# Starting the next pass in the first half of a gated-MLP unit: a two-layer decoder trunk on one core

## The chip, the cores and the metric

The kernel runs on one core of one Trainium2 chip. The metric is the device time of one execution in microseconds (us). Two layers run on 256 tokens, everything in 32-bit floats, with weights streamed once from memory.

## What is computed

Each of two layers is a mixer (gated spatial mixing and a gated recurrence in layer 0, forgetting attention in layer 1) followed by the gated MLP that the change is about:

```
def conv_ffn(h, w_up, conv_w, conv_b, w_down):
    seq = h.shape[1]
    z = h @ w_up                                   # 2048 -> 2 x 5632
    zp = jnp.pad(z, ((0, 0), (CONV_WIDTH - 1, 0), (0, 0)))
    z = sum(conv_w[j] * zp[:, j:j + seq] for j in range(CONV_WIDTH)) + conv_b
    a, b = jnp.split(z, 2, axis=-1)
    return (jax.nn.silu(a) * b) @ w_down           # 5632 -> 2048
```

with `x = x + conv_ffn(rms_norm(x), ...)` around it.

## The kernel before

**Numbers.** Every 32-bit factor is split into a high part and a remainder, and a product is three matmuls: high by high, high by remainder, remainder by high. For weights the split is done on the fly: a load of 512 KB on SyncE's queue (`weights`, L199) fills a buffer `w` (five of them), ScalarE copies its high part to `wh` (L186), VectorE subtracts to `wl` (L187), and TensorE may run.

**Pieces.** `project_four` makes four output blocks of 128 columns at a time for all 256 tokens, into two PSUM banks (one for each 128 tokens). It walks the inner dimension in *pieces* of 256: one load, one high part, one remainder, twelve matmuls of 512 columns (L380, L382, L383). Ahead of each piece it calls `tick()`, which moves a few waiting generators one step on; that is how evacuation, convolution and the rest are threaded between pieces.

**Ups.** `ffn` is a row of eleven *ups* a layer. An up makes four hidden tiles: its **first half** (`za`, the silu side) and its **second half** (`zb`, the linear side), each a `project_four` over 2048. After a half, `empty` evacuates two banks with the row scale (ScalarE L1422, into `z`), VectorE transposes in 32x32 blocks (L483), and 16 small moves of 32 KB, half on SyncE's queue and half on GpSimd's (L492), put the blocks in place in `zt`. Then `empty` lets LATE = 8 ticks go by before the convolution `conv` takes one of its four tiles at each tick: one tap with bias on ScalarE (L1436), one tap on ScalarE (L1437, into `tmp`), the middle tap on VectorE (L1438); then a closing add of all four (L1440). The first half ends with a silu, the second with the product of both sides (L1462) and a split into `hid` (L1466, L1468).

**Downs.** After three or two ups (STEPS) a *down* multiplies the hidden tiles made so far by `w_down`, in four `project_four` q = 0 to 3, added up in `y` (L1598, L1600). Ups run one or two ahead of what the down needs.

**The inset.** The first pieces of two neighbouring `project_four` (both halves of an up, or two q of a down) are done together by `seven`: seven block products (21 matmuls, L435 to L437) in place of eight (24 matmuls), at the price of sums of weights on VectorE (L448 to L451), of three and a half more weight splits, of sums of activations made once for each pass (`combos` in `combine`, L395 to L407), of two copies of a bank on ScalarE (L457, L462) and of two adds from PSUM on VectorE (L465, L470). `seven` is a generator in five steps and a rest: its two loads (L445), the sums, then the products. `project_four` drives it as its `inset`, one step ahead of each piece from the third on; two of its steps call `tick()` as well. It writes the four banks with which the next up or the next two q begin; those then skip their first piece ("begun").

**Where it stands.** In `up` the inset is handed to the second half: its seven pieces run with the start of the next up, or of the down when the up is the last before one. So a first half has 7 ticks (8 if not begun) and a second half 9. `combine(k0)` for a down is put in the queue of generators ahead of the last up before that down.

**Banks.** All eight PSUM banks are in use, four called `pm` and four `px`. `two_banks` hands out pairs, two pairs from one pool and two from the other in turn, so the four banks of a unit are a mixed set.

**Order.** The framework plans an order for each engine: by program order, but what it thinks is ready earlier may pass what it thinks is not. `held(r)` forbids `r` to go ahead of the last high part (or remainder) of a piece issued so far; it adds no wait on another engine. On the chip each engine then runs its instructions in that order, and waits where an operand is not there.

Of the kernel before, what the change touches and what calls it, by code (L numbers as in the profile page):

```python
# [8 lines left out]
F32 = mybir.dt.float32  # L9
# [6 lines left out]
P = 128  # L16
S = 256
D = 2048
KT = D // P
# [4 lines left out]
STEPS = ((3, 1), (3, 1), (3, 2), (2, 0))  # L24
BLK = 32
LAG = 6
LATE = 8
FORGET = 4
PAIR = 5
WAIT = 4  # L30
# [26 lines left out]
def tile_trunk(ctx: ExitStack, tc: tile.TileContext, x, pp_d, cst_d, mlev_d, msk_d,  # L57
# [295 lines left out]
                    deep["last"] = PE.matmul(to_two(ps[T]), al, h, start=False, stop=k + i == KT - 1)  # L353
        return ps

    def two_banks():
        ring[0] += 2
        pick = (lambda: pm.tile([P, 512], F32, tag="pm", name=nm("pm"))) if ring[0] % 8 < 4 else bank
        return [pick() for _ in range(2)]

    ring = [0]
    def project_four(w4, acts, n, k0=0, ks=None, ps=None, more=False, inset=None):

        begun = ps is not None
        loose = begun and "seven" in deep
        ps = ps or (two_banks() if "seven" in deep else
                    [pm.tile([P, 512], F32, tag="pm", name=nm("pm")) for _ in range(2)])
        ks = ks or range(0, n, 2)
        for k in ks:
            if inset is not None and (k - ks[0]) // 2 >= inset[1]:  # L370
                next(inset[0], None)
            tick()
            lo = (k0 + k) * P
            wh, wl = weights(w4[:, :, lo:lo + 2 * P].rearrange("m p c -> p m c"), 1024, 4)
            for T in range(2):
                for i in range(2):
                    a = acts(k + i) if callable(acts) else acts[k + i]
                    ah, al = a[:, T * P:(T + 1) * P], a[:, S + T * P:S + (T + 1) * P]
                    h, l = (by_rows(t, i) for t in (wh, wl))
                    PE.matmul(to_rows(ps[T]), ah, h, start=not begun and k + i == ks[0], stop=False,  # L380
                              skip_group_check=loose)
                    PE.matmul(to_rows(ps[T]), ah, l, start=False, stop=False, skip_group_check=loose)  # L382
                    deep["mm"] = deep["last"] = PE.matmul(to_rows(ps[T]), al, h, start=False,  # L383
                                                          stop=not more and k + i == ks[-1] + 1,
                                                          skip_group_check=loose)
        if inset is not None and inset[2]:
            for _ in inset[0]:
                pass
        return ps
# [1009 lines left out]
    def ffn(l, norm, last):  # L1399
# [10 lines left out]
            return (hp.tile([P, 1024], F32, tag="tmp", name=nm("tmp"), bufs=2),  # L1410
                    hp.tile([P, 4, S], F32, tag="zt", name=nm("zt"), bufs=2))

        def four(j0, inset=None, ps=None):
            ps = project_four(w_up[l, j0:j0 + 4], A, KT, ks=range(2 if ps else 0, KT, 2), ps=ps, inset=inset)
            tmp, zt = room()

            def empty():
                while norm.Rt is None:
                    yield
                z = [hp.tile([P, 512], F32, tag="z", name=nm("z"), bufs=2) for _ in range(2)]  # L1420
                for T in range(2):
                    SC.activation(cols4(z[T]), of_rows(ps[T]), AF.Copy, scale=norm.Rt[:, T:T + 1])  # L1422
                transposed(lambda T: z[T], tmp, zt)
                for _ in range(LATE):
                    yield

            return zt, tmp, empty()

        def conv(z4, tmp, j):
            c = hp.tile([P, 4, S], F32, tag="conv", name=nm("conv"), bufs=2)  # L1430
            far = tmp.rearrange("p (m t) -> p m t", m=4)
            for i in range(4):
                w = [pp[:, o:o + 1] for o in (C_CW + (l * 3 + n) * 2 * HT + j + i for n in range(3))]
                cb = C_CB + l * 2 * HT + j + i
                z, ci = z4[:, i], c[:, i]
                held(SC.activation(ci, z, AF.Identity, bias=pp[:, cb:cb + 1], scale=w[2]))  # L1436
                SC.activation(far[:, i], z, AF.Copy, scale=w[0])  # L1437
                V.scalar_tensor_tensor(ci[:, 1:], z[:, :S - 1], w[1], ci[:, 1:], ALU.mult, ALU.add)  # L1438
                yield
            held(V.tensor_tensor(c[:, :, 2:], c[:, :, 2:], far[:, :, :S - 2], ALU.add), "wl")  # L1440
            return c

        def up(j0, inset=None, begun=()):
            pa, pb = begun or (None, None)
            za, ta, ea = four(j0, None, pa)
            ca = []

            def gate():
                yield from ea
                a = yield from conv(za, ta, j0)  # L1450
                yield
                held(act(a, a, AF.Silu))
                ca.append(a)

            start(gate())
            zb, tb, eb = four(HT + j0, inset, pb)

            def fill():
                yield from eb
                b = yield from conv(zb, tb, HT + j0)  # L1460
                yield
                held(V.tensor_tensor(b, b, ca[0], ALU.mult), "wl")  # L1462
                t = hp.tile([P, 4, 512], F32R, tag="hid", name=nm("hid"), bufs=5)
                h, lo = (t[:, :, i * S:(i + 1) * S].rearrange("p m (t n) -> p m t n", t=2) for i in range(2))
                src = view(b, 0, (S, 4), (1, 2), (2, P))
                SC.activation(h, src, AF.Copy)  # L1466
                yield
                held(V.tensor_tensor(lo, src, h.bitcast(F32), ALU.subtract), "wl")  # L1468
                hid.extend(t[:, i] for i in range(4))

            start(fill())
# [68 lines left out]
        def begin(w4s, k, acts):  # L1540
            got = []

            def banks4():
                got.extend((two_banks(), two_banks()))
                return got

            def sums():
                while comb[0] != k:
                    tick()
                return right  # L1550

            spare = hp.tile([P, 512], F32, tag="z", name=nm("p5"), bufs=2)
            return got, seven(w4s, acts, lambda: comb[1], (k or 0) * P, banks4, sums, spare)
# [7 lines left out]
        def down(k0, n, first, final, begun, after):  # L1561
# [3 lines left out]
            for q in range(4):  # L1565
                if last and final and q == 3:
                    parts = None
                    for m in range(4 * q, KT):
                        end = m == KT - 1
                        ps = project(w_dn[l, m], acts, chunks=(n,), k0=k0, parts=parts)  # L1570
                        if not end:
                            tick()
                            parts = weights(w_dn[l, m + 1][:, k0 * P:(k0 + n) * P], n * P)
                        V.tensor_tensor(xT[m], xT[m], ps[:, 0:S], ALU.add)
                        finish_x(m)
                    return
                inset = ps = ks = None
                if not final:
                    ps, ks = begun[q % 2], range(2, n, 2)
                    if q == 0:  # L1580
                        later, gen = begin_down(2, k0)
                        inset = (gen, 2, False)
                    elif q == 1:
                        inset = (gen, 0, True)
                    elif q == 3 and after:
                        coming, gen = begin_up(j0)
                        inset = (gen, 0, True)
                ps = project_four(w_dn[l, 4 * q:4 * q + 4], acts, n, k0, ks=ks, ps=ps, inset=inset)
                if q == 1 and not final:
                    begun = later  # L1590
                    if after:
                        queue.append(combine(None))
                    else:
                        x_back()
                for T in range(2):
                    d = y[:, T, q * 512:(q + 1) * 512]
                    if first:
                        SC.activation(cols4(d), of_rows(ps[T]), AF.Copy)  # L1598
                    else:
                        V.tensor_tensor(cols4(d), cols4(d), of_rows(ps[T]), ALU.add)  # L1600
                if final:
                    add_y(q, True)
# [5 lines left out]
        for g, (now, ahead) in enumerate(STEPS):  # L1608
            until = sum(n for n, _ in STEPS[:g + 1]) + ahead
            while j0 < until:  # L1610
                now_begun, begun, inset = begun, (), None
                if j0 + 1 == until:
                    queue.append(combine(k0))
                    begun, gen = begin_down(0, k0)
                    inset = (gen, 2, True)
                elif j0:
                    begun, gen = begin_up(j0 + 1)
                    inset = (gen, 2, True)
                up(4 * j0, inset, now_begun)
                j0 += 1  # L1620
            n, final = 4 * now, g == len(STEPS) - 1
            while len(hid) < k0 + n:
# [94 lines left out]
```

## Time and profile before

| | |
|---|---|
| device time, median of 3 runs | 2194.82 us (2188.66 to 2194.99) |
| the profiled execution, its own time | 2194.9 us |
| its span, first to last instruction | 2193.1 us |
| VectorE busy | 1750.2 us (80%) |
| ScalarE busy | 1428.8 us (65%) |
| bytes moved, mean rate | 491.99 MB, 224 GB/s |
| the gated MLP's weight loads, issued | 346.8 to 1038.6 us (layer 0), 1483.4 to 2176.1 us (layer 1) |

A row of the windows view gives a stretch in us from the span's start, its length, and the busy time of each engine with the number of its instructions in brackets. A row of the timeline gives start, duration, engine, line and operands; in square brackets stands how long the engine sat idle before it, and what ended that. A row of the waits view gives who waited for whom: us in total, times, longest. TensorE's matmuls overlap: each is shown with some 0.38 us while they start 0.22 us apart, so its busy share says little about small losses.

### The profile page before, as it was taken

The numbers are of one execution on the slowest core, as the hardware profiler recorded it, in microseconds if no ns is written. First come the engines' busy times: TensorE is split into PE (matmuls) and PEld (weight loads), VectorE is DVE, ScalarE is ACT, GpSimd is POOL, SyncE is SP. The second block draws the span as 40 slices with busy tenths as digits, with TensorE's granted clock in tenths as the row PEclk, the third lists the DMA queues.
The fourth block names the chain that finished last, engine by engine and source line by source line (L and its number), as shares of the span: only waits on it lengthen the run. The fifth ranks groups of instructions, "written<-read, shape, count | busy, mean of one in ns | idle before, by whom it ended". The sixth has DMA issues, their size and how long they took to land.

```text
span 2193.1 us, 32450 instructions
## 1 busy us (share of the span) xinstructions
PE 2158.5 (98%) x10646; PEld 1879.4 (86%) x10646; DVE 1750.2 (80%) x2373; ACT 1428.8 (65%) x2064; POOL 480.6 (22%) x873
## 2 busy tenths in 40 slices
PE   9999999999999999999999999999999999999999
PEld 8888888888888887888888888888788888888888
DVE  7888768778768967886987887877788778877986
ACT  6677766676667656774666556766677567657762
POOL 0352231212012001210233443222121021011202
PEclk9999999999999999999999999999999999999999
DMA  8755778867777766677777766787777767677796
GB/s 297 220 173 174 230 222 263 241 190 209 231 218 222 233 221 192 208 242 243 250 238 222 242 206 207 217 264 235 217 220 232 238 190 223 205 224 231 208 289 190
DMA packets 494345, 491.99 MB, mean 224 GB/s; under 512 B 115584, under 2 KB 460304, under 8 KB 494048
## 3 DMA queue, kind: packets, MB, share of 16 engines
q1 hardware_dynamic: 466752, 457.60, 66.6%
q0 software_dynamic: 25984, 30.18, 5.7%
q10 hardware_dynamic: 1440, 2.15, 0.3%
q8 instruction: 83, 1.36, 0.3%
q14 instruction: 86, 0.70, 0.1%
HBM read 439.44 MB, written 6.31 MB: 203 GB/s over the span
## 4 chain that ended last, share of the span: by engine, by line
PE 72%; DVE 10%; DMA 9%; SPq 4%; issue 3%; ACT 2%; DVEq 0%; POOL 0%; ACTq 0%; POOLq 0%
PE pm L382 11%; PE pm L380 11%; PE pm L383 11%; DMA w<-in_w_up 6%; PE px L382 5%; PE px L383 5%; PE px L380 5%; DVE wl L187 5%; PE pm L351 4%; PE pm L353 4%; PE pm L352 4%; SPq L492 3%; DMA w<-in_w_dn 2%; DVE tmp L483 1%; PE pm L237 1%
## 5 line engine op out<-in xcount | busy, mean ns | idle before, releaser
L187 DVE TENSOR_TENSOR wl<-w,wh 128x1024 fp32r<-128x1024 f32 (+1 forms) x790 | 950.4, 1217 | 319.1 <-ACT wh L186 317.4
L186 ACT ACTIVATE wh<-w 128x1024 fp32r<-128x1024 f32 (+1 forms) x790 | 818.2, 1049 | 466.8 <-PE pm L383 132.5
L492 POOL DMA_DIRECT2D zt<-tmp x413 | 224.3, 551 | 1143.4 <-DVE tmp L483 836.7
L382 PE MATMUL pm<-wl,a 128*128 128x512 f32 x952 | 364.2, 383 | 8.2 <-DVE wl L187 8.2
L380 PE MATMUL pm<-wh,a 128*128 128x512 f32 x952 | 363.1, 381 | 0.1
L383 PE MATMUL pm<-wh,a 128*128 128x512 f32 x952 | 361.9, 380 | 0.0
L382 PE MATMUL px<-wl,a 128*128 128x512 f32 x632 | 241.5, 382 | 5.6 <-DVE wl L187 5.5
L380 PE MATMUL px<-wh,a 128*128 128x512 f32 x632 | 240.3, 380 | 0.0
L383 PE MATMUL px<-wh,a 128*128 128x512 f32 x632 | 240.0, 380 | 0.0
L382 PEld LDWEIGHTS pm<-wl,a 128*128 128x128 f32 x952 | 180.7, 190 | 39.4 <-DVE wl L187 14.2
L380 PEld LDWEIGHTS pm<-wh,a 128*128 128x128 f32 x952 | 180.5, 190 | 26.3 <-ACT wh L186 0.5
L383 PEld LDWEIGHTS pm<-wh,a 128*128 128x128 f32 x952 | 180.8, 190 | 25.4
L351 PE MATMUL pm<-wh,a 128*128 128x512 f32 x416 | 158.5, 381 | 0.0
L352 PE MATMUL pm<-wl,a 128*128 128x512 f32 x416 | 157.7, 379 | 0.0
L353 PE MATMUL pm<-wh,a 128*128 128x512 f32 x416 | 157.7, 379 | 0.0
L382 PEld LDWEIGHTS px<-wl,a 128*128 128x128 f32 x632 | 119.9, 190 | 27.5 <-DVE wl L187 10.7
L1436 ACT ACTIVATE conv<-zt,pp 128x256 f32<-128x256 f32 x176 | 104.8, 595 | 52.2 <-DMA zt<-tmp 38.4
L380 PEld LDWEIGHTS px<-wh,a 128*128 128x128 f32 x632 | 120.0, 190 | 17.2
L383 PEld LDWEIGHTS px<-wh,a 128*128 128x128 f32 x632 | 119.7, 189 | 16.8
L492 POOL DMA_DIRECT2D turn<-tmp x159 | 86.7, 553 | 184.1 <-DVE tmp L483 162.4
L382 PE MATMUL px<-wl,hid 128*128 128x512 f32 x304 | 115.6, 380 | 0.7 <-DVE wl L187 0.7
L187 DVE TENSOR_TENSOR wl<-sums,wh 128x1024 fp32r<-128x1024 f32 (+1 forms) x90 | 94.2, 1046 | 26.8 <-ACT wh L186 26.8
(334 smaller groups left out, 3949.8 us busy)
## 6 DMA issues: line engine op xcount, KB each, us to landing
w<-in_w_up SPq DMA_DIRECT2D x334, 512.0 KB, 5.9
w<-in_w_dn SPq DMA_DIRECT2D x164, 512.0 KB, 5.6
w<-in_w_cqkv SPq DMA_DIRECT2D x96, 512.0 KB, 5.2
w<-in_w_abo SPq DMA_DIRECT2D x32, 512.0 KB, 5.0
w<-in_w_cg SPq DMA_DIRECT2D x32, 512.0 KB, 5.5
w<-in_w_co SPq DMA_DIRECT2D x32, 512.0 KB, 5.3
zt<-tmp SPq DMA_DIRECT2D x416, 32.0 KB, 2.2
zt<-tmp POOLq DMA_DIRECT2D x413, 32.0 KB, 2.0
```

The source lines that it names most:

```text
L186: r = deep["wh"] = SC.activation(wh, w, AF.Copy)
L187: deep["wl"] = V.tensor_tensor(wl, w, wh.bitcast(F32), ALU.subtract)
L237: deep["last"] = PE.matmul(to_two(ps[g][T]), a[:, o + T * P:o + (T + 1) * P], by_two(t, i), start=k + i + j == 0, stop=k + i == KT - 1 and ...
L351: PE.matmul(to_two(ps[T]), ah, h, start=k + i == 0, stop=False)
L352: PE.matmul(to_two(ps[T]), ah, l, start=False, stop=False)
L353: deep["last"] = PE.matmul(to_two(ps[T]), al, h, start=False, stop=k + i == KT - 1)
L380: PE.matmul(to_rows(ps[T]), ah, h, start=not begun and k + i == ks[0], stop=False, skip_group_check=loose)
L382: PE.matmul(to_rows(ps[T]), ah, l, start=False, stop=False, skip_group_check=loose)
L383: deep["mm"] = deep["last"] = PE.matmul(to_rows(ps[T]), al, h, start=False, stop=not more and k + i == ks[-1] + 1, skip_group_check=loose)
L483: r = V.transpose(tmp.rearrange("p (b m i t) -> p b m i t", b=4, m=4, t=2)[:, :, :, :, T], src(T).rearrange("p (m b j) -> p b m j", m=4, b=4))
L492: queues[(a + b) % len(queues)].dma_start(dst[BLK * b:BLK * (b + 1), :, a * n:(a + 1) * n], tmp[BLK * a:BLK * (a + 1), b * 4 * n:(b + 1) * ...
L1436: held(SC.activation(ci, z, AF.Identity, bias=pp[:, cb:cb + 1], scale=w[2]))
```

## The change

The inset moves from the second half of an up to the first. All four banks of an up are taken at its start, and banks are handed out by fours, all `pm` or all `px` in turn; a `project_four` that gets fresh banks is told so (`fresh`). The combination for a down is put in the queue in the middle of the second-last up before it, behind its inset, and no longer at the start of the last up. The convolution waits nine ticks, not eight. The ScalarE tap L1437 is held like L1436.

```diff
-LATE = 8
+LATE = 9
...
-    def two_banks():
-        ring[0] += 2
-        pick = (lambda: pm.tile([P, 512], F32, tag="pm", name=nm("pm"))) if ring[0] % 8 < 4 else bank
-        return [pick() for _ in range(2)]
+    def four_banks():
+        ring[0] += 1
+        pick = (lambda: pm.tile([P, 512], F32, tag="pm", name=nm("pm"))) if ring[0] % 2 else bank
+        return [[pick() for _ in range(2)] for _ in range(2)]
...
-    def project_four(w4, acts, n, k0=0, ks=None, ps=None, more=False, inset=None):
-
-        begun = ps is not None
+    def project_four(w4, acts, n, k0=0, ks=None, ps=None, more=False, inset=None, fresh=False):
+
+        begun = ps is not None and not fresh
         loose = begun and "seven" in deep
-        ps = ps or (two_banks() if "seven" in deep else
-                    [pm.tile([P, 512], F32, tag="pm", name=nm("pm")) for _ in range(2)])
+        ps = ps or [pm.tile([P, 512], F32, tag="pm", name=nm("pm")) for _ in range(2)]
...
-        def four(j0, inset=None, ps=None):
-            ps = project_four(w_up[l, j0:j0 + 4], A, KT, ks=range(2 if ps else 0, KT, 2), ps=ps, inset=inset)
+        def four(j0, inset, ps, begun):
+            ps = project_four(w_up[l, j0:j0 + 4], A, KT, ks=range(2 if begun else 0, KT, 2), ps=ps, inset=inset,
+                              fresh=not begun)
...
-                SC.activation(far[:, i], z, AF.Copy, scale=w[0])
+                held(SC.activation(far[:, i], z, AF.Copy, scale=w[0]))
...
-        def up(j0, inset=None, begun=()):
-            pa, pb = begun or (None, None)
-            za, ta, ea = four(j0, None, pa)
+        def up(j0, inset=None, begun=(), after=None):
+            pa, pb = begun or four_banks()
+            za, ta, ea = four(j0, inset, pa, begun)
+            if after is not None:
+                queue.append(after)
...
-            zb, tb, eb = four(HT + j0, inset, pb)
+            zb, tb, eb = four(HT + j0, None, pb, begun)
...
-                got.extend((two_banks(), two_banks()))
+                got.extend(four_banks())
...
-                inset = ps = ks = None
+                inset = ks = None
+                if not q % 2:
+                    pair = begun or four_banks()
+                ps = pair[q % 2]
                 if not final:
-                    ps, ks = begun[q % 2], range(2, n, 2)
+                    ks = range(2, n, 2)
...
-                now_begun, begun, inset = begun, (), None
+                now_begun, begun, inset, then = begun, (), None, None
                 if j0 + 1 == until:
-                    queue.append(combine(k0))
                     begun, gen = begin_down(0, k0)
                     inset = (gen, 2, True)
                 elif j0:
                     begun, gen = begin_up(j0 + 1)
                     inset = (gen, 2, True)
-                up(4 * j0, inset, now_begun)
+                if j0 + 2 == until:
+                    then = combine(k0)
+                up(4 * j0, inset, now_begun, then)
```

More of the change, by code (lines that the diff above doesn't have):

```diff
@@ L1587, in down @@
                         inset = (gen, 0, True)
-                ps = project_four(w_dn[l, 4 * q:4 * q + 4], acts, n, k0, ks=ks, ps=ps, inset=inset)
+                ps = project_four(w_dn[l, 4 * q:4 * q + 4], acts, n, k0, ks=ks, ps=ps, inset=inset,
+                                  fresh=final)
                 if q == 1 and not final:
```

## The prediction

> **What bounds the kernel now.** I begin with the page's first part, then ask who made TensorE wait.
>
> ```profile
> PE 2158.5 (98%) x10646; PEld 1879.4 (86%) x10646; DVE 1750.2 (80%) x2373; ACT 1428.8 (65%) x2064; POOL 480.6 (22%) x873
> ```
> ```profile
> PE pm L382 <- DVE wl L187: 8.7, 11, 2.3
> PE px L435 <- ACT px L457: 8.5, 2, 4.7
> PE px L382 <- DVE wl L187: 6.3, 8, 1.6
> PE pm L435 <- ACT pm L457: 3.6, 3, 2.6
> ```
>
> TensorE has nearly no room: the change takes no matmul away, so all it can win is waits. They are of two kinds: a matmul with a weight remainder waits for VectorE (8.7 + 6.3 us), and a product of the inset waits for ScalarE's copy L457 (8.5 + 3.6 us). Both lie in the ups. How much an up loses in all, a window from evacuation to evacuation shows better, because a busy matmul is drawn with 0.38 us and issued every 0.216:
>
> ```profile
> 788.00:827.90 39.90, 39.90 (x186) 34.95 (x185) 27.92 (x32) 23.97 (x30) 4.34 (x8) 1.00 0.74 234
> ```
> ```profile
> 402.03:452.64 50.61, 47.50 (x210) 40.37 (x209) 38.92 (x46) 33.48 (x49) 8.70 (x16) 0.97 0.72 216
> ...
> 492.05:537.09 45.04, 42.74 (x190) 36.82 (x189) 37.66 (x49) 31.08 (x44) 8.69 (x16) 0.96 0.70 210
> ...
> 827.90:875.72 47.82, 43.17 (x190) 37.18 (x189) 35.23 (x41) 30.90 (x42) 8.69 (x16) 0.93 0.73 219
> ...
> 1538.16:1590.27 52.11, 47.51 (x210) 40.38 (x209) 38.88 (x46) 33.62 (x48) 8.70 (x16) 0.97 0.69 210
> ...
> 2045.81:2087.44 41.63, 41.28 (x191) 35.60 (x190) 36.78 (x48) 30.96 (x45) 8.69 (x16) 1.00 0.65 192
> sum 696.01, PE 671.94 PEld 578.18 DVE 567.51 ACT 493.87 POOL 139.03; mean PE 42.00 PEld 36.14 DVE 35.47 ACT 30.87 POOL 8.69
> ```
>
> The first fence is the first up behind a down: 186 matmuls, no idle, so 39.90 / 185 = 0.2157 us from start to start. It and its three sisters lose nothing. The second fence is the other sixteen ups with an inset: 696.01 us for 3065 matmuls (210, 181, then 190 or 191 each, in both layers). Less one at each window's edge, 3049 x 0.2157 = 657.7 us: the **pool is 38.3 us**. Three windows hold half of it: 50.61 - 45.1 = 5.5, 47.82 - 40.8 = 7.0 and 52.11 - 45.1 = 7.0, together **19.5**; thirteen others share **18.8**, of which the one at 492 has 4.3.
>
> Now the halves of two ups (first half of the up at work, second, and again):
>
> ```profile
> 638.90:661.00 22.10, 22.10 (x104) 19.36 (x103) 13.66 (x16) 13.41 (x19) 4.34 (x8) 1.00 0.63 189
> 661.00:681.50 20.50, 19.08 (x88) 16.17 (x87) 20.35 (x24) 16.79 (x25) 4.34 (x8) 1.00 0.77 237
> 681.50:704.30 22.80, 22.80 (x107) 19.96 (x107) 16.62 (x25) 14.63 (x21) 4.34 (x8) 1.00 0.73 224
> 704.30:724.40 20.10, 18.50 (x86) 15.65 (x85) 20.07 (x24) 16.39 (x25) 4.34 (x8) 1.00 0.50 141
> ```
>
> The fourth figure is VectorE: 13.66 of 22.10 and 16.62 of 22.80 in first halves, 20.35 of 20.50 and 20.07 of 20.10 in second halves. Over an up VectorE has room; in the half with the inset it has none, and there TensorE idles.
>
> The three dear windows have another cause, on ScalarE (timeline, then TensorE's for the same place, then for the window at 492):
>
> ```profile
> 865.00 0.60 ACT L1436 ACTIVATE conv<-zt,pp 128x256 f32<-128x256 f32 x1 [5.34 <-DMA zt<-tmp]
> 865.51 0.49 ACT L1437 ACTIVATE tmp<-zt,pp 128x256 f32<-128x256 f32 x1
> 865.91 1.04 ACT L186 ACTIVATE wh<-sums 128x1024 fp32r<-128x1024 f32 x1
> 866.85 0.58 ACT L457 ACTIVATE px<-px 128x512 f32<-128x512 f32 x1
> ```
> ```profile
> 867.48 0.80 PE L435 MATMUL px<-wh,a 128*128 128x512 f32 x1 [4.65 <-ACT px L457]
> 868.07 0.63 PE L436 MATMUL px<-wl,a 128*128 128x512 f32 x1
> 868.50 0.63 PE L437 MATMUL px<-wh,a 128*128 128x512 f32 x1
> ```
> ```profile
> 523.01 0.48 PE L382 MATMUL pm<-wl,a 128*128 128x512 f32 x1 [2.30 <-DVE wl L187]
> ...
> 524.32 0.63 PE L383 MATMUL pm<-wh,a 128*128 128x512 f32 x1
> ```
>
> The first convolution tap of the first half's tiles stands at the eighth tick, ahead of two instructions of the inset that need nothing from it. Its `zt` has not landed, ScalarE sits 5.34 us, and the copy L457 with TensorE behind it waits. After such a stop matmuls start 0.43 us apart for some 4 us (868.07, 868.50): a second bill of about 2 us.
>
> The Trainium skill, page "TensorE: Matmul & The Clock Gate", Part 1, puts the half rate behind an idle window of about 3.4 us. The row at 523.01 shows it already after 2.30 us; by the rule that window would win some 2 us less than I credit, by the row it wins them.
>
> **Part by part.** *The inset into the first half.* Instructions and loads are the same; their neighbours change. With the inset a half has 9 ticks, without it 7. Before: the first half's taps come at ticks 8 and 9 of the second half and 1, 2 of the next first half; the second half's taps, add, multiply L1462 and split L1468 at ticks 1 to 7 of the next second half, all beside the inset. After, with nine ticks: the first half's taps at ticks 2 to 5 of the next first half, add at 6; the second half's first tap at tick 9, the rest, add, multiply and split in ticks 1 to 6 of the second half, which has no inset.
>
> ```profile
> L1438 DVE SCALAR_TENSOR_TENSOR conv<-zt,pp,conv 128x255 f32<-128x255 f32 x176 | 84.2, 480 | 27.8 <-ACT conv L1436 27.8
> ...
> L1440 DVE TENSOR_TENSOR conv<-conv,tmp 128x1016 f32<-128x1016 f32 x44 | 52.6, 1195 | 0.0
> L1468 DVE TENSOR_TENSOR hid<-conv,hid 128x1024 fp32r<-128x1024 f32 x22 | 33.5, 1522 | 0.1
> L1462 DVE TENSOR_TENSOR conv<-conv,conv 128x1024 f32<-128x1024 f32 x22 | 26.9, 1221 | 0.0
> ```
>
> In the half with the inset VectorE now carries six taps, one add, multiply and split: 2.9 + 1.2 + 1.2 + 1.5 = 6.8 us. After, five taps and one add: 3.6. So 3.2 us leave a half whose VectorE time is 20.1 to 20.4 of 20.1 to 20.5, and go to one with 13.7 to 16.6 of 22. That makes some 17 of 20.5 in the one and 17 to 20 of 22 in the other: a tenth to spare in each. What it wins is less than 3.2, since much of what leaves stands behind the stop:
>
> ```profile
> 661.12 1.23 DVE L187 TENSOR_TENSOR wl<-w,wh 128x1024 fp32r<-128x1024 f32 x1 [2.91 <-ACT wh L186]
> 662.26 1.56 DVE L483 STREAM_TRANSPOSE tmp<-z 128x512 f32<-128x512 f32 x2
> 663.66 0.47 DVE L1438 SCALAR_TENSOR_TENSOR conv<-zt,pp,conv 128x255 f32<-128x255 f32 x1
> ...
> 665.22 1.24 DVE L1440 TENSOR_TENSOR conv<-conv,tmp 128x1016 f32<-128x1016 f32 x1
> ...
> 667.70 2.35 DVE L187 TENSOR_TENSOR wl<-w,wh 128x1024 fp32r<-128x1024 f32 x2
> ```
>
> Between the remainder at 661.12 and the late one at 667.70 stand transposes, one tap, the four sums and the closing add. After, transposes and sums still do, with two taps and no add: 1.24 + 0.47 - 0.96 = 0.75 us less. Over thirteen windows that is 9.8 at most; some lose no more than 0.6, and the stop at 523 may fall below the length that brings the half rate (2 us): I take **9**, with ends of 0 and 18.8.
>
> *Nine ticks.* Now the second half's tap is the one that might find no `zt`. Its place is one tick later, behind the high part of the inset's third weights and, I expect, the copy L457. Ahead of the wait then go 1.04 + 0.58 us of ScalarE work and about one piece of 12 x 0.2157 = 2.6: 4.2 of the 5.34 us. The two other places:
>
> ```profile
> 437.44 0.60 ACT L1436 ACTIVATE conv<-zt,pp 128x256 f32<-128x256 f32 x1 [5.67 <-DMA zt<-tmp]
> ```
> ```profile
> 1575.08 0.60 ACT L1436 ACTIVATE conv<-zt,pp 128x256 f32<-128x256 f32 x1 [6.88 <-DMA w<-in_w_up]
> ```
>
> (At 1575 the view names a load; the line waits for its `zt`.) Less 4.2 each, 1.1, 1.5 and 2.7 stay, 5.3 of 19.5: **14**, with ends of 0 and 19.5.
>
> *Queues.* The two loads of the inset (L445, 512 KB each) stay in the first third of a half, behind the 16 moves of the half before; SyncE gives its eight 5.11 us:
>
> ```profile
> 663.85 5.11 SPq L492 DMA_DIRECT2D zt<-tmp  x8
> ```
>
> Their order against moves and loads is the same in either half: nothing, and bounded by the 2.91 us (row at 661.12) for which VectorE waits there now, either way. *The held tap*: nothing; taps of 0.49 us (865.51) that ran ahead of a high part no longer may, up to three in a row, -1.5 to +1.5 us. *Banks by fours*: the inset's second product needs a bank evacuated at the end of the half before, four pieces or 10 us earlier; without that cover one copy of a bank, 0.58 us (866.85), a unit, 12 in all. *Combination earlier*: its 3.0 us (16.62 less 13.66) go from one half without inset to another: nothing; without cover 3.0 x 6. *Downs*: the six first units of a down have an inset of their own and get two more taps, 0.96 us, but no longer follow a saturated half. I charge **3** (0.5 x 6), ends -5 and +6.
>
> Sum: -14 - 9 + 3 = -20 from the profiled execution's 2194.9 us (span 2193.1 and 1.8 around it; the runs' median is 2194.82, the same): **2175 us**.
>
> **Rivals.** (1) *The wait moves with the unit.* The second half's `zt` is late as the first's was, and what of ScalarE is late next is the second copy L462. For it: moves that GpSimd issues beside the loads are slow, whatever the half:
>
> ```profile
> 858.29 6.56 DMA zt<-tmp
> ```
> ```profile
> zt<-tmp POOLq DMA_DIRECT2D x413, 32.0 KB, 2.0
> ```
>
> The chain has one at 6.56 us, the page's median is 2.0. The Trainium skill, page "DMA: Bandwidth & Descriptors", section "Issuing engines are not separate DMA queues", says the same: all queues interleave on the same 16 engines. Against it: one tick more. The 14 fall away: -9 + 3 = -6, 2189. (2) *It doesn't do what it says*: the planner puts sums and taps where they stood, and only the 3 us of the downs move: 2192 to 2198. (3) *Slower*: the wait meets every unit. Place: ScalarE, at tick 9, ahead of the last high parts of the inset. It decides as soon as `zt` lands later than ScalarE gets there in most ups; now it does in three of twenty. Price: the 14 not won, and 2 us in ten of the others, less 6 from above: +14, **2209**.
>
> **How the numbers follow.** Forecast (2175, own range 2158 to 2188) 0.64; rival 1 0.15; rival 2 0.08; rival 3 0.13. A measurement of this kernel tells about 0.3%, 6.6 us, from no change. Faster by more: 0.64; within: 0.15 + 0.08 = 0.23; slower: 0.13. The range goes from 2158 (pool nearly emptied: 2194.9 - 38.3 = 2156.6) to 2198, which takes in rivals 1 and 2 and leaves out rival 3 and some 0.05 below.
>
> **What would show it.** Windows between evacuations near 41 us in all twenty ups; VectorE 80 to 90% in both halves. The wait of L435 for L457 gone, with the half-rate matmuls. Wrong if ScalarE's first tap still sits for microseconds in the half with the inset, if the remainder in front of the first block product is as late as at 667.70, or if downs lose what ups win.

## The result and the profile after

| | before | after |
|---|---|---|
| device time, median of 4 runs on one chip | 2191.86 us (2188.66 to 2194.99) | 2156.24 us (2154.89 to 2157.13) |
| ratio to before, 95% interval | | 0.9837 [0.9817, 0.9858] |
| the profiled execution, its span | 2194.9, 2193.1 us | 2157.13, 2155.3 us |

The change makes the kernel 36 us (1.6%) faster. The forecast was 20 us, and the time lies 1.8 us below its range. In the kernel after, pieces and products stand one line earlier than before (L382 is L381, L435 is L434, L457 is L456), and multiply and split two later (L1462 is L1464, L1466 is L1468). Two single runs far above their sisters (4618.19 us in held_late9, 2235.52 us in load_in_second) are left out of the medians and ratios below.

The page after, its first part and the chain that ended last; then the chain of before:

```profile
PE 2144.4 (99%) x10646; PEld 1876.6 (87%) x10646; DVE 1747.0 (81%) x2373; ACT 1424.7 (66%) x2064; POOL 477.9 (22%) x873
...
PE 90%; DVE 4%; DMA 3%; issue 1%; SPq 1%; ACT 1%; DVEq 0%; ACTq 0%; POOLq 0%
```
```profile
PE 72%; DVE 10%; DMA 9%; SPq 4%; issue 3%; ACT 2%; DVEq 0%; POOL 0%; ACTq 0%; POOLq 0%
```

The same work, done by the same number of matmuls: busy times of VectorE and ScalarE move by 3 and 4 us. The chain now is TensorE itself for nine tenths. TensorE's waits after, those in the ups (two others are of 1.1 and 0.2 us):

```profile
PE px L381 <- DVE wl L187: 2.6, 4, 1.7
PE pm L381 <- DVE wl L187: 2.4, 3, 1.3
```

The 15.0 us of waits for remainders are 5.0, and the 12.1 us for ScalarE's copy of a bank are gone. By windows, evacuation to evacuation (three of fourteen ups with an inset, and the sum of the fourteen; the last row shown has few matmuls because the window ahead of it holds more, 199):

```profile
611.77:653.09 41.32, 41.32 (x193) 36.18 (x192) 30.84 (x37) 28.93 (x40) 8.66 (x16) 1.00 0.70 206
653.09:693.88 40.79, 40.79 (x191) 35.72 (x190) 36.76 (x49) 30.86 (x44) 8.65 (x16) 1.00 0.75 232
...
1950.73:1991.85 41.12, 39.87 (x185) 34.37 (x184) 34.84 (x42) 30.11 (x43) 8.66 (x16) 1.00 0.69 206
sum 582.05, PE 578.33 PEld 502.93 DVE 482.74 ACT 420.33 POOL 121.26; mean PE 41.31 PEld 35.92 DVE 34.48 ACT 30.02 POOL 8.66
```

These fourteen hold 2692 matmuls, less one each 2678, which at 0.2157 us is 577.6: 4.4 us lost, 0.3 an up, where before each lost 2.4 (38.3 over sixteen). The granted clock, the third figure from the end, is 1.00 in all fourteen; it was 0.93 to 0.97 in the dear ones. The halves of two ups; the inset is now in the second and the fourth row:

```profile
611.80:632.30 20.50, 20.50 (x97) 17.95 (x96) 12.81 (x14) 12.65 (x17) 4.33 (x8) 1.00 0.85 251
632.30:653.10 20.80, 20.80 (x98) 18.22 (x97) 18.00 (x24) 16.25 (x25) 4.33 (x8) 1.00 0.56 162
653.10:672.90 19.80, 19.80 (x94) 17.33 (x93) 17.52 (x24) 13.48 (x19) 4.32 (x8) 1.00 0.90 280
672.90:693.90 21.00, 21.00 (x99) 18.40 (x98) 19.25 (x25) 17.39 (x28) 4.33 (x8) 1.00 0.61 186
```

VectorE has 18.00 of 20.80 and 19.25 of 21.00 us in the half with the inset, where it had 20.35 of 20.50. ScalarE at an inset after (timeline):

```profile
643.87 0.58 ACT L456 ACTIVATE pm<-pm 128x512 f32<-128x512 f32 x1
644.38 0.58 ACT L1436 ACTIVATE conv<-zt,pp 128x256 f32<-128x256 f32 x1
...
646.73 0.60 ACT L461 ACTIVATE p<-pm 128x512 f32<-128x512 f32 x1 [1.37 <-PE pm L436]
```

The copy L456 goes ahead of the first tap, as the prediction had it, and the tap does not wait. Where one still does, no matmul waits for the copy (the first tap's own view: ScalarE's idle time ahead of it, us and times, by what ended it):

```profile
  DMA w<-in_w_up: 8.1, 3
  DMA zt<-tmp: 5.5, 1
  issue: 3.7, 1
```

Of these waits (of 5.5, 5.3, 2.4 and 3.7 us, the small rest apart) the first three are for the first-half tiles that made the three dear windows of before (402, 828 and 1538); they are late still, but now the tap stands where no copy is behind it. The fourth is for a second half's tile.

Where the 36 us came from, told by the starts of matmuls in the two traces (what each gap has beyond 0.216 us, added up by the number of the matmul): in the two gated MLPs TensorE lost 46.5 us before and 9.8 after. The three dear windows gave 5.0, 6.9 and 7.1, together 19.0; the thirteen other ups of the prediction 12.5, from 0.1 to 2.1 each; the downs 5.2, from 0.1 to 1.4 in each stretch of them. So the ups are the place, as forecast, and the downs win too, which was not. What earned it is another matter, and the experiments are about that.

### The profile page after: what moved, and what is told of

It reads as the page before. It is cut to its first block, busy times and chain, and to the rows that moved or that the text cites. A ratio compares the mean times of both kernels' runs of the same rounds, so it can differ in the third digit from the quotient of the medians.

```text
span 2155.3 us, 32486 instructions
## 1 busy us (share of the span) xinstructions
PE 2144.4 (99%) x10646; PEld 1876.6 (87%) x10646; DVE 1747.0 (81%) x2373; ACT 1424.7 (66%) x2064; POOL 477.9 (22%) x873
## 4 chain that ended last, share of the span: by engine, by line
PE 90%; DVE 4%; DMA 3%; issue 1%; SPq 1%; ACT 1%; DVEq 0%; ACTq 0%; POOLq 0%
PE pm L381 13%; PE pm L379 13%; PE pm L382 13%; PE px L381 8%; PE px L382 8%; PE px L379 8%; PE pm L351 5%; PE pm L352 4%; PE pm L353 4%; DMA w<-in_w_up 2%; DVE wl L187 2%; PE pm L237 1%; PE pm L316 1%; PE pm L434 1%; PE pm L435 1%
## 5 line engine op out<-in xcount | busy, mean ns | idle before, releaser
L381 PE MATMUL pm<-wl,a 128*128 128x512 f32 x952 | 361.7, 380 | 2.4 <-DVE wl L187 2.4
L382 PE MATMUL pm<-wh,a 128*128 128x512 f32 x952 | 360.8, 379 | 0.0
L381 PE MATMUL px<-wl,a 128*128 128x512 f32 x632 | 240.2, 380 | 2.4 <-DVE wl L187 2.3
L382 PE MATMUL px<-wh,a 128*128 128x512 f32 x632 | 239.5, 379 | 0.0
L381 PEld LDWEIGHTS pm<-wl,a 128*128 128x128 f32 x952 | 179.9, 189 | 30.4 <-DVE wl L187 5.3
L382 PEld LDWEIGHTS pm<-wh,a 128*128 128x128 f32 x952 | 179.9, 189 | 25.2
L381 PEld LDWEIGHTS px<-wl,a 128*128 128x128 f32 x632 | 119.4, 189 | 21.4 <-DVE wl L187 4.6
L382 PEld LDWEIGHTS px<-wh,a 128*128 128x128 f32 x632 | 119.4, 189 | 16.8
L381 PE MATMUL pm<-wl,hid 128*128 128x512 f32 x304 | 115.4, 380 | 0.0
L379 PE MATMUL pm<-wh,hid 128*128 128x512 f32 x304 | 115.2, 379 | 0.0
L382 PE MATMUL pm<-wh,hid 128*128 128x512 f32 x304 | 115.2, 379 | 0.0
```

## The experiments

All runs are of the whole kernel on one core; each ratio is to the kernel before on the same chip in the same batch, by three or more runs of either. The intervals carry the scatter of the kernel before (2188.55 to 2203.29 us in one batch, say). The variants of the change scatter less: its own runs lie at 2154.89 to 2157.13, those of full_late10 at 2160.50 to 2162.79, of taps_in_a_row at 2162.35 to 2164.11, of silu_later at 2156.29 to 2157.27. So 5 us between two of these are told from their own times, though their ratios' intervals touch; but they ran on several chips.

| run | median, us | ratio to before, 95% | us to before |
|---|---|---|---|
| late9_alone | 2204.70 | 1.0053 [1.0038, 1.0068] | +12 |
| held_alone | 2189.73 | 0.9981 [0.9971, 0.9991] | -4 |
| held_late9 | 2188.16 | 0.9969 [0.9951, 0.9987] | -6 |
| banks_alone | 2192.39 | 1.0001 [0.9984, 1.0017] | +1 |
| inset_alone | 2169.01 | 0.9891 [0.9869, 0.9914] | -24 |
| full_but_unheld | 2167.80 | 0.9883 [0.9868, 0.9898] | -25 |
| full_but_late8 | 2162.10 | 0.9857 [0.9840, 0.9873] | -31 |
| the change | 2156.24 | 0.9837 [0.9817, 0.9858] | -36 |
| full_late10 | 2161.03 | 0.9853 [0.9836, 0.9869] | -32 |
| silu_later | 2156.99 | 0.9831 [0.9816, 0.9846] | -36 |
| taps_in_a_row | 2163.11 | 0.9860 [0.9845, 0.9874] | -30 |
| load_in_first | 2164.08 | 0.9868 [0.9852, 0.9884] | -30 |
| load_in_second | 2162.32 | 0.9862 [0.9846, 0.9879] | -32 |
| handoff_in_first | 2173.06 | 0.9906 [0.9878, 0.9934] | -19 |
| same_work_no_handoff | 2163.19 | 0.9865 [0.9835, 0.9894] | -29 |
| handoff_in_second | 2154.81 | 0.9820 [0.9791, 0.9850] | -37 |
| before_without_handoff | 2200.02 | 1.0033 [1.0022, 1.0044] | +7 |

### Part by part: which edit earns what

**Nine ticks alone**, in the kernel before.

```diff
-LATE = 8
+LATE = 9
```

> The kernel before with LATE = 9 and nothing else. Two causes (mine): the ninth tick alone ends ScalarE's waits of 5 to 7 us in front of the copy of the first product, but VectorE stays full in the second half: 10 to 17 us faster, and the matmuls with a remainder go on waiting for VectorE (15 us in the waits view before). One cause, balance of VectorE: under 5 us. Interaction: without the move of the inset the ninth tick only pushes taps deeper into the full half: 0, or some us slower.

It is 12 us slower. What the edit was to do, it did: ScalarE's idle time ahead of the first tap falls from 52.2 us to 9.3 (the line's own view, before and in this run):

```profile
  DMA zt<-tmp: 38.4, 21
  DMA w<-in_w_up: 13.8, 2
```
```profile
  issue: 5.2, 2
  DMA zt<-tmp: 2.7, 2
  DMA w<-in_w_up: 1.4, 1
```

The loss came from elsewhere (TensorE's and ScalarE's waits, then ScalarE's timeline at an inset):

```profile
PE pm L382 <- DVE wl L187: 10.8, 13, 1.8
PE px L382 <- DVE wl L187: 10.1, 12, 2.2
PE pm L435 <- ACT pm L457: 5.4, 5, 1.6
PE px L435 <- DVE pm L465: 4.4, 2, 3.7
...
ACT hid L1466 <- DVE conv L1462: 54.7, 17, 5.8
```
```profile
669.83 1.39 ACT L1466 ACTIVATE hid<-conv 128x1024 fp32r<-128x1024 f32 x1 [4.54 <-DVE conv L1462]
671.12 0.58 ACT L457 ACTIVATE pm<-pm 128x512 f32<-128x512 f32 x1
671.63 1.04 ACT L186 ACTIVATE wh<-sums 128x1024 fp32r<-128x1024 f32 x1
```

The reader sees a queue in order at work. One tick later, the second half's multiply (VectorE L1462) and its high part (ScalarE L1466) come into the middle of the inset. ScalarE reaches L1466 and sits 4.54 us until VectorE, behind its remainders, has multiplied; the copy L457 and a high part of the inset's sums, ready or nearly so, stand behind it. Such waits came to 54.7 us; before they were

```profile
ACT hid L1466 <- DVE conv L1462: 29.8, 18, 2.1
```

The wait for a transfer has made room for a wait on a neighbour engine. TensorE's waits are 5.9 us longer for remainders than before, and its products wait 6.9 us for adds from PSUM, where it was 0.9; for the copy they wait less, 8.9 us (one row of 3.5 is not shown) where it was 12.1. And VectorE, the fourth figure, isn't fuller: between the evacuations around this place it now has 20.99 of 22.60 us, 93%, where the kernel before had 20.35 of 20.50:

```profile
657.40:680.00 22.60, 21.19 (x96) 17.30 (x95) 20.99 (x25) 16.89 (x26) 4.33 (x8) 1.00 0.70 213
```

**The held tap alone, with nine ticks, and the banks alone**, in the kernel before.

```diff
-                SC.activation(far[:, i], z, AF.Copy, scale=w[0])
+                held(SC.activation(far[:, i], z, AF.Copy, scale=w[0]))
```

> The kernel before with the ScalarE tap held and nothing else. Balance (now mine: what counts is VectorE's load in the half with the inset, and the held tap only keeps a high part from waiting behind taps): 0 to 6 us faster than before, since the second half stays full. Order: the held tap ends ScalarE's waits wherever the inset is: 7 us faster or more. Neither: no change.

> The kernel before with the held tap and LATE = 9, the inset still in the second half. Balance: still slower than before, by 3 to 12 us, as with LATE = 9 alone (12 us slower): the late tap puts two taps more behind the inset in the full half. Order: at least 5 us faster than before.

> The kernel before with banks handed out by fours, all four of an up at its start; inset, combination, ticks and tap as before. All theories: within 3 us of the kernel before. A cost or gain of over 6 us would make the banks a part of the change of their own, which the prediction put at nothing.

The held tap is worth 4 us alone, and turns the +12 of nine ticks into -6; for the latter the expectation by order was right and the one by balance, 3 to 12 us slower, was not. The banks (`four_banks` and `fresh`, without the inset's move) are worth nothing.

**The inset's move alone** (the change with eight ticks and the tap free), and the change without one or the other:

```diff
-LATE = 9
+LATE = 8
...
-                held(SC.activation(far[:, i], z, AF.Copy, scale=w[0]))
+                SC.activation(far[:, i], z, AF.Copy, scale=w[0])
```

> The inset in the first half with its banks by fours and its earlier combination, but LATE = 8 and the ScalarE tap not held. Two causes: the waits for VectorE go, the wait of ScalarE for the convolution's tile stays (now that of the second half's tiles, in two to four ups): 12 to 20 us faster. One cause, balance: 28 us faster or more, near the full change. Interaction: under 8 us, since the tap then stands one tick earlier than in the full change and the inset's copies queue behind it.

> The full change with LATE = 8. Two causes: 8 to 18 us slower than the full change, with ScalarE sitting for microseconds in front of a first tap in some of the halves with the inset. One cause, balance: within 4 us of the full change.

> The full change with the ScalarE tap L1437 not held. Two causes: within 3 us of the full change, as the prediction put the held tap at nothing. Rival: the held tap is the third part of the gain, because three taps in a row ahead of a high part delay the remainder behind it: 5 to 12 us slower than the full change, as waits of matmuls for VectorE.

So all eight cells stand, in us against before: none 0, nine ticks +12, held -4, both -6; with the move -24, with nine ticks -25, held -31, both -36. The move is worth 24 to 37 in every row of it. Nine ticks are worth 1 to 5 beside the move. The hold is worth 4 in the kernel before and 7 to 18 beside the move, nine ticks or both; some of these steps are no larger than the intervals allow, the signs of the large ones are sure. The 24 us of the move alone, and the 6 us that the change loses without its ninth tick, lie between the ranges expected for them.

Where the move alone wins is told by the starts of matmuls, one trace of each. At the three dear windows inset_alone loses 1.0 us of the 19.7 that the kernel before loses; at the thirteen other ups 15.9 of 18.9; in the downs 6.3 of 6.5. So 18.7 of its 22 us are the three dear windows, with eight ticks and the tap free. Their tiles, the first halves', are about as late as before: ScalarE sits 5.79, 6.43 and 5.68 us in front of them. But a weight's high part stands behind that tap now, not the inset's copy, and TensorE idles nowhere in that up (ScalarE's timeline, the window around it):

```profile
856.83 0.60 ACT L1436 ACTIVATE conv<-zt,pp 128x256 f32<-128x256 f32 x1 [6.43 <-DMA sums<-in_w_up]
...
858.62 1.04 ACT L186 ACTIVATE wh<-w 128x1024 fp32r<-128x1024 f32 x1
```
```profile
820.16:862.30 42.14, 42.14 (x197) 36.86 (x196) 33.90 (x40) 29.39 (x42) 8.65 (x16) 1.00 0.79 238
```

(At 856.83 the view names a load; the line waits for its `zt`.) In all ScalarE idles longer than before ahead of its first tap, 88.7 us where it was 52.2, and the kernel is 24 us faster all the same (the largest part of it in the line's view, and the timeline at an inset):

```profile
  DMA zt<-tmp: 76.8, 36
```
```profile
643.93 0.60 ACT L1436 ACTIVATE conv<-zt,pp 128x256 f32<-128x256 f32 x1 [2.46 <-DMA zt<-tmp]
...
644.84 0.57 ACT L456 ACTIVATE pm<-pm 128x512 f32<-128x512 f32 x1
...
646.78 1.29 ACT L1437 ACTIVATE tmp<-zt,pp 128x256 f32<-128x256 f32 x3
```

So by these rows what counts isn't how long ScalarE waits, but what stands behind the tap. The last row shows what the hold forbids: three taps in one go ahead of the copy L461 and three high parts.

**All four taps in a row, but held**, in the kernel after: the tap of the first tick takes all four tiles.

```diff
-                held(SC.activation(far[:, i], z, AF.Copy, scale=w[0]))
+                if i == 0:
+                    for n in range(4):
+                        o = C_CW + l * 3 * 2 * HT + j + n
+                        held(SC.activation(far[:, n], z4[:, n], AF.Copy, scale=pp[:, o:o + 1]))
```

> The full change with all four ScalarE taps of a half issued, held, at the first of its four ticks, so four in a row (2 us) stand ahead of the next high part. Row (the held tap gains because it breaks up rows of taps): 6 to 12 us slower than the full change, as without holding. Place (it gains because an unheld tap may pass the copy or a high part of an earlier step): within 3 us of the full change.

7 us slower than the change by the medians, 5 by what each gains on the kernel before; the hold is worth 12 or 11 there. All taps are held in both kernels; the rows of them are what differs. So about half of what the hold buys is that taps come one to a piece; for the other half no run shows the reason.

### Amount or order: is VectorE the bound?

The prediction read the gain as VectorE getting air in the half with the inset. If the amount decides, more work for VectorE in that half must cost far more than in the other. Eight adds that nobody reads, 3.3 us, ahead of pieces of each first half (or second half) of the ups with an inset, in the kernel after:

```diff
+            if deep.get("load") and 1 <= (k - ks[0]) // 2 <= 4:
+                for _ in range(2):
+                    sq = tp.tile([P, S], F32, tag="sq", name=nm("sq"))
+                    held(V.tensor_tensor(sq, pp[:, 0:S], pp[:, S:2 * S], ALU.add), "wl")
```

> The full change with eight adds of 128 x 256 on VectorE (0.42 us each, 3.3 us, about what the move takes from the half with the inset) at pieces 2 to 5 of every first half that has an inset; their result is not used. Balance: 15 to 40 us slower than the full change (20 halves, 3.3 us less a slack of one to two), as waits of matmuls for VectorE. Order or queues: within 5 us of the full change, as nothing changes place.

> The same eight adds at pieces 2 to 5 of the second half of the same ups, which has no inset; their result is not used. Balance: within 5 us of the full change, since that half has some 4 us of VectorE to spare. Order or queues: the same cost as in the first half, whatever it is.

Twenty times 3.3 are 66 us of work on VectorE, and they cost 8 us in the first half and 6 in the second (6 and 4 by what each gains on the kernel before). That is between the ranges of the two theories, and nearly the same in either half. It isn't yet the full half of the kernel before: VectorE runs ahead of TensorE, so of the eight adds of a first half only four lie between the evacuations that bound the half with the inset. There VectorE has 95% (this run; 19.25 of 21.00 in the change):

```profile
673.00:694.50 21.50, 21.12 (x98) 18.18 (x98) 20.48 (x29) 17.49 (x28) 4.33 (x8) 1.00 0.62 185
```

Then the order. A stand-in for the multiply, the high part and the remainder is put where they stood before, or where they stand now: three adds on VectorE, three copies on ScalarE that read the result, three subtractions on VectorE that read the copies.

```diff
+            at = (k - ks[0]) // 2
+            if deep.get("load") and at == 4:
+                s1, s2 = (tp.tile([P, S], F32, tag="sq", name=nm("sq")) for _ in range(2))
+                for _ in range(3):
+                    held(V.tensor_tensor(s1, pp[:, 0:S], pp[:, S:2 * S], ALU.add), "wl")
+                for _ in range(3):
+                    held(SC.activation(s2, s1, AF.Copy))
+            if deep.get("load") and at == 5:
+                for _ in range(3):
+                    held(V.tensor_tensor(s1, pp[:, 0:S], s2, ALU.subtract), "wl")
```

In same_work_no_handoff the copies read a constant in place of `s1`; in handoff_in_second the chain stands in the second half, one piece later (`at == 5` and `6`).

> The full change with a stand-in for the chain that the move takes out of the half with the inset (multiply on VectorE, high part on ScalarE that waits for it, remainder on VectorE that waits for that): in every first half with an inset three adds of 128 x 256 on VectorE and three copies of their result on ScalarE at piece 5, three subtractions of that on VectorE at piece 6; the result is not used. Handoff (mine now: two engines in order that wait for each other in front of the inset's splits are what the move takes away): 15 to 30 us slower than the full change, most of the gain of the inset alone (24 us). Amount (a few us more on each engine, order without effect): 5 to 10 us slower, as the adds of the runs before cost 8.

> The same six VectorE and three ScalarE instructions at the same places, but each reads a constant, so neither engine waits for the other; the result is not used. Handoff: at most 10 us slower than the full change and at least 8 us faster than with the handoff. Amount: the same as with the handoff, within 3 us.

> The chain with the handoff at pieces 6 and 7 of the second half of the same ups, behind the kernel's own; the result is not used. Handoff: at most 10 us slower than the full change, as no inset's splits queue behind it. Amount: as in the first half, within 3 us.

In the half with the inset the chain costs 17 us, the same instructions without the waits between the engines 7, and the chain in the second half, a piece later, nothing (-1). The trace of handoff_in_first, lines ten higher than after (ScalarE's timeline, TensorE's waits):

```profile
646.48 1.32 ACT L378 ACTIVATE sq<-sq 128x256 f32<-128x256 f32 x3 [1.21 <-DVE sq L376]
647.70 1.04 ACT L186 ACTIVATE wh<-sums 128x1024 fp32r<-128x1024 f32 x1
648.65 0.58 ACT L466 ACTIVATE pm<-pm 128x512 f32<-128x512 f32 x1
```
```profile
PE pm L391 <- DVE wl L187: 6.2, 11, 1.4
PE px L391 <- DVE wl L187: 3.5, 8, 1.1
PE pm L444 <- ACT pm L466: 2.0, 4, 0.7
PE px L444 <- ACT px L466: 1.9, 3, 0.8
```

A wait of 1.21 us ahead of a high part and the copy; TensorE's waits for the copy, which the change had taken away, are back. In same_work_no_handoff the rows for remainders are 5.5 and 2.0, and the copy is waited for once, 0.5. So by the medians some 10 of the 17 us are the handoff and 7 the work.

The run without the handoff also shows what a full VectorE costs. Of its sixteen halves with an inset between two evacuations eleven have VectorE at 99%, as twelve have in the kernel before:

```profile
674.97:695.56 20.59, 19.06 (x88) 16.06 (x87) 20.43 (x29) 18.18 (x30) 4.34 (x8) 1.00 0.49 143
```

By the starts of matmuls these eleven lose 10.6 us, and the same halves of the change 5.5; the twelve of the kernel before lose 14.7. So a full half loses 1 us or so in either kernel, and half of that where VectorE has air. The amount has a price, but it explains neither the three dear windows nor late9_alone, where VectorE is at 93%.

### Which waits count

**Ten ticks**, in the kernel after.

```diff
-LATE = 9
+LATE = 10
```

> The full change with LATE = 10. Room (the ninth tick gains because the moved blocks have landed by then): 0 to 3 us faster than the full change, whose trace still has two first taps that wait 5 us. Place (nine is where add and silu fall between the inset's steps): 3 to 12 us slower.

It is 5 us slower than the change. ScalarE's idle time ahead of the first tap is all but gone (1.0 and 0.4 us), but the copy, for which nobody waits in the change, is waited for again, and the waits ahead of silu and high part have grown (TensorE's waits, ScalarE's):

```profile
PE px L434 <- ACT px L456: 2.1, 3, 1.0
...
PE pm L434 <- DVE pm L464: 1.2, 2, 0.8
...
ACT conv L98 <- DVE conv L1440: 58.9, 20, 3.6
ACT hid L1468 <- DVE conv L1464: 23.3, 19, 2.2
```

**Silu three ticks later**, in the kernel after, whose largest new wait is ScalarE's silu for the closing add.

```diff
-                yield
+                for _ in range(4):
+                    yield
```

> The full change with the silu three ticks later, so that it falls into the second half. Handoff: the 47.9 us that ScalarE sits in front of the silu in the half with the inset (22 times, for VectorE's closing add) go, and of the 10 us that the two MLPs still lose 2 to 6 go with them. Amount: within 2 us of the full change.

In the change ScalarE's waits have the row

```profile
ACT conv L98 <- DVE conv L1440: 47.9, 20, 2.8
```

and with the later silu the 47.9 us are not there any more. The time is the same (+0.8): they cost nothing. Here the handoff was expected to cost 2 to 6 us and doesn't, so a wait of one engine for another in the half with the inset is not dear as such.

**The kernel before with the high part of `hid` on VectorE**, so that the handoff falls away.

```diff
-                SC.activation(h, src, AF.Copy)
+                V.tensor_copy(h, src)
```

> The kernel before with the high part of the hidden tiles (L1466) made on VectorE in place of ScalarE, all else as before: the handoff VectorE to ScalarE to VectorE is gone from the half with the inset, ScalarE loses 1.5 us and its wait of 1.7 us there (29.8 us in 18 waits), and VectorE gets about 1.2 us more in the half that reads 20 of 20 us. Handoff: 4 to 15 us faster than the kernel before. Amount (that half is full of VectorE work, and that is what costs): 10 us slower or more.

It is 7 us slower, between the two ranges expected (lines as before; TensorE's waits and ScalarE's):

```profile
PE px L382 <- DVE wl L187: 8.9, 12, 1.7
PE pm L382 <- DVE wl L187: 8.3, 12, 1.8
PE px L435 <- ACT px L457: 7.8, 2, 4.8
...
ACT conv L1436 <- DMA zt<-tmp: 51.7, 27, 6.2
```

The 29.8 us of waits ahead of the high part are gone, TensorE's waits are as before, and ScalarE waits for `zt` instead, 51.7 us where it was 38.4. This kernel gives VectorE 22 times 0.81 us more, so it doesn't say what the handoff alone cost before; it says that taking it away there, at the price of that work, brings nothing. A longer delay that moves the handoff without adding work needs further buffers and wasn't tried.

## Why the prediction was right and wrong

**Right.** The place (the ups, with the three dear windows at the head), the sign, the copy L457 out of TensorE's waits, the half rate gone with it, the banks, and the second half as a place with room for multiply and split (handoff_in_second). Rival 1, that the second half's tile is late next, is seen in one place: in inset_alone ScalarE sits 5.67 us for it at 1954.79, a product waits for the copy and TensorE loses 3.0 us; in the change ScalarE sits 3.7 us for the same tile and no product waits for the copy.

**"Nine ticks: 14".** This step failed. Its 14 us are the three dear windows, and it gave them to the ninth tick because, once the inset has moved, "the second half's tap is the one that might find no `zt`". With the inset moved and eight ticks the three places lose 1.0 us of 19.7: the late tiles are still the first halves', and the move by itself takes the copy out from behind them. The ninth tick alone costs 12 us. The mechanism that the step named is there (52.2 us of ScalarE's idle time fall to 9.3), but a tick of delay shifts the whole convolution: multiply and high part came to stand ahead of the copy, and the step asked only for what is ahead of the tap. Even with 76.8 us of such idle time for `zt` alone the move alone is 24 us faster, so idle ScalarE was a poor measure of what its wait costs. In the change the three windows gave 19.0, not 14.

**"I take 9" for the inset's move.** The move is 24 alone and up to 37 beside the other edits, so as the price of an edit this term is the furthest off. But 18.7 of the 24 are the three dear windows. At the thirteen other ups, for which the 9 were meant, the move alone wins 3.0, and the whole change 12.5. The step counted 3.2 us of VectorE work that leave a full half and priced 0.75 us of it ahead of the late remainder. Its premise, that VectorE's fill decides, holds in part at most: a full half loses about 1 us again in same_work_no_handoff, but in late9_alone most halves at 93% lose 2 us or more, and in the change VectorE got less air than forecast (18.0 and 19.3 us of work, not 17) while TensorE lost less. The stand-in adds a second price, that of the handoff from VectorE to ScalarE and back in the middle of the inset, 10 us; in the second half, which has no inset, it costs nothing. The move alone takes that chain out of the inset and wins only 3.0 us at these ups, so the handoff explains little of the 24, unless the move put something as dear in its place. Why the hold and the ninth tick win 9.5 more there, once the inset has moved, stays open.

**"The held tap: nothing", -1.5 to +1.5.** It is 4 alone, 7 beside the move, 11 with nine ticks as well. The step saw the row of three taps (0.49 us each) and priced it by ScalarE's work; the cost is what stands behind the row, a copy and high parts that a remainder and TensorE wait for.

**"Downs: I charge 3".** They gained 5.2 us by the starts of matmuls. That they "no longer follow a saturated half" isn't what won it, for with the move alone they still lose 6.3 of 6.5 us. In the change they lose 1.3, without its hold 7.7.

**Banks, combination, queues: nothing.** The banks are shown (2192.39 against 2191.73). The combination and the two loads were not run by themselves; no wait in the trace after names them.

The sum was -14 - 9 + 3 = -20. By place it came out as -19.0 - 12.5 - 5.2. By edits it is: move -24, and -12 more for hold and nine ticks, which are worth that only beside it. The parts don't add up; each of them shifts what the others put side by side in a queue. The low end was too high because it stood on an emptied pool of ups alone: some 8 of the 46.5 us lost before lay outside those sixteen windows. (It was also put at 2158, where that pool gives 2156.6.)

No version run here is clearly faster than the change: handoff_in_second, with work that nobody needs, and silu_later are level with it.

## What to carry to other kernels

Before a delay or a move is priced, write out the new order in each engine's queue and look for an instruction that waits ahead of one that the bottleneck needs. Here three transfers stayed late, and the move won 18.7 us because the copy no longer stood behind them; a handoff put in front of the inset's splits cost 10 us over twenty ups on top of its work, and nothing in the half without the inset. An engine at 99% in a window is not thereby the bound: here a half at 99% lost about 1 us. Add work to it and see where the work lands. And run the parts of a change alone and together: here one part changes sign (nine ticks, +12 alone, -2 with the hold).

## What the runs showed of the hardware

Two things had not been expected. The kernel before varies by 0.3% in four runs on one chip (2188.66 to 2194.99 us) and by 0.7% in thirteen on another (2188.55 to 2203.29), while the change keeps to 0.1% in its four (2154.89 to 2157.13). A kernel full of waits on slow transfers spreads more than one whose chain is TensorE for 90%: that is a reading of two kernels, not a tested rule. And VectorE ran so far ahead of TensorE that work put into one half by the program was half done in the window of the half before: of eight adds in a first half four lay between the evacuations that bound it, where VectorE's time rose from 19.25 of 21.00 us to 20.48 of 21.50. All eight, in twenty ups, cost 8 us. A window cut at TensorE's evacuations is not the same stretch of VectorE's program.
